# Head 1's scores ahead of the last query tile, and the sample's second value product behind the first transposition

## Chip, cores and metric

The kernel runs on one core of a Trainium2 chip. The metric is the device time of one execution in microseconds (us); the lower, the better.

## What is computed

One step of a decoder trunk of two layers, in fp32, for a prompt of 512 rows and a sample of 8 sequences of 4 new rows each; the model width is 1024, with 8 heads of 128. The second layer has the attention that the change touches. Cut to that:

```python
q = rmsnorm((xn @ att_w_q[j]).reshape(bsz, L, N_HEADS, HEAD_DIM), q_norm[j])
# prompt, per head, in blocks of 128 queries
s = einsum('bqhd,bkhd->bhqk', qb, k) * scale + cq[..., :, None] - csum[..., None, :]
p = softmax(where(causal, s, -inf));  o = einsum('bhqk,bkhd->bqhd', p, v)
# sample: 256 past keys from a paged cache and 4 new ones
p = softmax(concatenate([s_past, s_new], axis=-1))
o = einsum(p[..., :P], v_past) + einsum(p[..., P:], v_new)
mix = o.reshape(bsz, L, D_ATT) @ att_w_o[j]
```

The trunk around it (feed-forward pairs, a gated token mixer, a gated per-layer input) returns the prompt's and the sample's rows, keys, values and log forget values.

## The kernel before

All activations lie transposed on chip, 128 features by 544 columns: 512 of the prompt and 32 of the sample. A product of full precision is made of three products of split operands: each operand is cast into a high half by ScalarE (L279) and VectorE computes the rest by subtraction (L280); the same pair of lines prepares queries, turned probabilities and head outputs.

The attention is written as a list of steps, `ORDER` (L58), which a loop calls one by one. A scheduler then orders the instructions of each engine. It may move them against the list, except where an instruction is kept in program order (`keep_in_program_order`). `self.pins` says for how many of the next products the first matmul is kept so. DMA requests go out on SyncE's queue in order.

The steps that matter here, with a head, a tile or a group behind the letter:

- **q** is one query tile: 48 products of a weight block with the input (L235, L239, L241), its eviction (L949), and the square of it on ScalarE (L697).
- **s** (`s0123`, `s4567`) are the statistics of four heads: column sums of the squares on TensorE with a matrix of ones (L705), a reciprocal square root on ScalarE of each half (L334), three steps on VectorE (L337, L340, L341), and DMAs that write the rows (L716). **n** reads a head's row back, broadcast over the partitions (L721), and multiplies (L959).
- **f** requests the keys and values of a head (L992, L993); **p** splits its queries (L279, L280).
- **a** scores a head: 20 products (L1007 to L1015) into two score tiles, then for each of four query blocks of 128 the maximum on VectorE (L1025), Exp with its sum on ScalarE (L1026), the reciprocal (L1027) and the scaling on ScalarE or GpSimd (L1031, L1029). The key widths of the four blocks are 128, 256, 384 and 512. The two tiles are buffers that the next scores need, too.
- **t** turns the probabilities by ten transpositions (L1041) and splits them; **v** is the value product of 12 matmuls (L1059 to L1061), split into the head's output.
- **K**, **V**, **z**, **S**, **T** prepare the sample's keys, values, queries, scores and turned probabilities. **P** (`P0`, `P1`) is the sample's value product of a group of four sequences: 24 matmuls of 32 rows, L1124 for the past and L1129 for the new rows; eight VectorE steps (L1137, L1139) then mask the heads and sum them into one tile. **U** transposes that tile (L1143), kept in program order; **O** spreads it.
- **h** (`h00` to `h31`) is half an output projection of the first 272 columns (L1167, L1170, L1171), evicted by L1181; **o** is the projection of the other 272 columns.

There are three PSUM buffers of two banks, "ps" (query tiles, scores, turned blocks, the sample's value products, projections), and two of one bank, "pb" (square sums, the rest of a turn, value products, transpositions). The functions Exp and reciprocal square root stand in different tables of ScalarE, and an `ACT_TABLE_LOAD` changes the table.

Of the kernel before, what the change touches and what calls it, by code (L numbers as in the profile page):

```python
# [29 lines left out]
P = 128  # L30
# [10 lines left out]
NH = 8  # L41
# [16 lines left out]


ORDER = """  # L60
q0 K3 K2 K0 q1 q2 q3 K1 s0123 n2 n3 n1 q4 f1 p1 q5 q6 f0 n0 q7 p2 p0 f3 f2 a0 s4567 p3 t0 a1 v0 a2
t1 n4 a3 t2 p4 n5 n7 n6 z f4 K5 v1 v2 f5 p5 K6 t3 a4 S0 v3 f6 h00 p6 V5 f7 a5 K7 t4 K4 v4 t5 p7 V7
V3 v5 a6 x V2 h10 t6 a7 V4 S1 t7 T0 v6 V0 V1 v7 h20 V6 h30 T1 P0 h01 U0 P1 O0 h11 U1 O1 h21 h31 o0 o1 o2
o3 o4 o5 o6 o7
"""
# [18 lines left out]
def whole(p):  # L84

    return p[:].rearrange("p a b -> p (a b)")[:, 512 - CUT:512 - CUT + T]


class Builder:
# [845 lines left out]
    def queries(self, xs, acc):  # L935

        nc = self.nc
        q, sqs, bcs, box = {}, {}, {}, {}

        def tile(h):  # L940
            if h == 0:
                p, box["rstd"] = self.tile_rstd(xs, acc)
            else:
                p = self.tile_mm(xs)
            if h % 2 == 0:
                box["q"] = self.big()

            def take(p=p, qc=box["q"][:, h % 2, :]):
                box["last"] = nc.vector.tensor_tensor(qc, whole(p), box["rstd"], ALU.mult)  # L949
                q[h], sqs[h] = qc, self.square(qc)  # L950
            self.evac(take)

        def stat(*hs):
            bcs.update(zip(hs, self.head_rows([sqs.pop(h) for h in hs], P ** -0.5)))

        def norm(h):
            bc = bcs.pop(h)()
            with self.tc.issue_after(box["last"].ins):
                nc.vector.scalar_tensor_tensor(q[h], q[h], self.gain(G_Q), bc, ALU.mult, ALU.mult)  # L959
        return q, tile, stat, norm  # L960
# [21 lines left out]
    def attention(self, xs, acc, h_out, on_chunk):  # L982
        nc = self.nc
# [134 lines left out]
        def sample_pv(g):  # L1118
            pt = st.pop(("pt", g))
            acc = self.ps()  # L1120
            for a in range(2):
                for pg in range(NPAGE):
                    for b4 in range(4):
                        nc.tensor.matmul(acc[32 * b4:32 * b4 + 32, a, :],  # L1124
                                         pt[:, pg * P + 32 * b4:pg * P + 32 * b4 + 32],
                                         self.pages["V", 4 * g + b4, pg][:, a, :], start=pg == 0, stop=False,
                                         skip_group_check=True)
                for b4 in range(4):
                    nc.tensor.matmul(acc[32 * b4:32 * b4 + 32, a, :],  # L1129
                                     pt[:NS, 256 + 32 * b4:256 + 32 * b4 + 32],  # L1130
                                     st["vs"][:NS, a, :], start=False, stop=True, skip_group_check=True)
            st["oh", g] = oh = self.tmp()[:, :P]
            for h in range(NH):
                src = acc[:, h // 4, (h % 4) * P:(h % 4) * P + P]
                m = self.c[:, C_H + h:C_H + h + 1]
                if h == 0:
                    nc.vector.tensor_scalar(oh, src, m, None, ALU.mult)  # L1137
                else:
                    nc.vector.scalar_tensor_tensor(oh, src, m, oh, ALU.mult, ALU.add)  # L1139
# [45 lines left out]
        def project(c):  # L1185
# [7 lines left out]

        do = dict(q=tile, s=stat, n=norm, f=fetch, p=prep_q, a=qk, t=turn, v=pv, K=self.load_k, V=self.load_v,
                  z=sample_q, S=sample_qk, T=sample_turn, P=sample_pv, U=sample_back, O=sample_out, x=load_vs, h=project_half,
                  o=project)
        for step in ORDER.split():
# [214 lines left out]
```

## Time and profile before

| | us |
|---|---|
| median of 3 runs | 2075.44 |
| lowest to highest | 2074.86 to 2076.22 |
| the profiled execution, its own time | 2074.3 |
| its span in the trace | 2072.5 |
| TensorE busy in the span | 2043.4 (99%) |
| VectorE busy | 1509.7 (73%) |
| ScalarE busy | 941.7 (45%) |

The span begins with the first and ends with the last instruction; 1.8 us of the execution lie around it. Starts in the trace are counted from the span's start. PE is TensorE, DVE is VectorE, ACT is ScalarE, POOL is GpSimd, SP is SyncE. Of a matmul the start is known better than the end, so neighbours overlap on the timeline; an idle time stands in brackets in front of the instruction that ended it, with the engine that released it. The granted clock (PEclk) is a share of 2.4 GHz: 1.00 is that level and 0.50 is 1.2 GHz.

### The profile page before, as it was taken

The page shows a single profiled execution, that of the slowest core. Times are in us where ns is not written, and L with a number is a line of the kernel's source. Part 1 is how long each engine was busy: PE and PEld are TensorE (multiplying, and loading weights), DVE is VectorE, ACT ScalarE, POOL GpSimd, SP SyncE. Part 2 cuts the span into 40 slices and gives each one's busy share as a digit, 9 for nine tenths or more (in the row PEclk, how much of TensorE's full clock was granted, in tenths as well). Part 3 has the DMA queues.
Part 4 walks back from the last instruction along what each step waited for, and adds up shares of the span by engine and source line. Part 5 has one row for each costly group of instructions (what it writes and reads, how often), then busy time and mean ns, then how long its engine had stood idle before and what let it go on. Part 6 is the DMA issues. An engine that isn't in the chain of part 4 may idle for free. (4 is left out here: it accounts for less than half of the span.)

```text
span 2072.5 us, 38744 instructions
## 1 busy us (share of the span) xinstructions
PE 2043.4 (99%) x16388; PEld 2015.6 (97%) x16388; DVE 1509.7 (73%) x1874; ACT 941.7 (45%) x1389; POOL 180.9 (9%) x230
## 2 busy tenths in 40 slices
PE   8999999999999999999999999999999999999999
PEld 8999999999999999999999999999987999999999
DVE  7877777556687778776697777776476788777773
ACT  6535344423554434454355443534364654343451
POOL 0000000300100000052050000001142200000020
PEclk9999999999999999999999999999999999999999
DMA  5223224212223232422193323324668322322431
GB/s 184 91 104 111 74 102 155 82 44 86 87 83 113 72 112 92 140 91 92 50 333 129 112 85 110 110 67 130 198 206 305 102 102 74 111 101 84 130 96 44
DMA packets 93887, 237.94 MB, mean 115 GB/s; under 512 B 9602, under 2 KB 27554, under 8 KB 93714
## 3 DMA queue, kind: packets, MB, share of 16 engines
q1 hardware_dynamic: 93570, 235.42, 33.9%
q8 instruction: 129, 2.11, 0.4%
q14 instruction: 44, 0.36, 0.1%
q10 hardware_dynamic: 144, 0.04, 0.0%
HBM read 218.94 MB, written 16.49 MB: 114 GB/s over the span
## 5 line engine op out<-in xcount | busy, mean ns | idle before, releaser
L480 PE MATMUL ps<-big,big 128*128 128x272 f32 x5616 | 729.9, 289 | 8.1 <-DVE big L497 4.8
L480 PEld LDWEIGHTS ps<-big,big 128*128 128x128 f32 x5616 | 715.8, 189 | 9.5 <-issue 5.3
L193 DVE TENSOR_TENSOR big<-big,big 128x1024 fp32r<-128x1024 f32 (+2 forms) x538 | 590.4, 1099 | 113.7 <-ACT big L192 112.5
L192 ACT CAST big<-big 128x1024 fp32r<-128x1024 f32 (+2 forms) x538 | 488.1, 932 | 267.7 <-DVE big L178 260.2
L235 PE MATMUL ps<-big,big 128*128 128x256 f32 (+1 forms) x2832 | 590.0, 289 | 9.6 <-ACT big L192 7.0
L239 PE MATMUL ps<-big,big 128*128 128x256 f32 (+1 forms) x2832 | 584.8, 287 | 0.0
L241 PE MATMUL ps<-big,big 128*128 128x256 f32 (+1 forms) x2832 | 584.0, 288 | 0.0
L235 PEld LDWEIGHTS ps<-big,big 128*128 128x128 f32 x2832 | 453.8, 189 | 12.7 <-ACT big L192 7.0
L239 PEld LDWEIGHTS ps<-big,big 128*128 128x128 f32 x2832 | 457.0, 189 | 0.0
L241 PEld LDWEIGHTS ps<-big,big 128*128 128x128 f32 x2832 | 453.4, 188 | 0.7 <-issue 0.4
L320 POOL TENSOR_TENSOR st<-st,tmp 128x544 f32<-128x544 f32 (+1 forms) x63 | 87.2, 1384 | 1622.9 <-ACT tmp L318 1622.7
L519 DVE SCALAR_TENSOR_TENSOR big<-ps,big 128x544 f32<-128x544 f32 x160 | 115.6, 723 | 106.5 <-PE ps L241 106.3
L178 DVE TENSOR_TENSOR big<-big,big 128x1024 f32<-128x1024 f32 x156 | 190.2, 1219 | 0.3 <-DMA big<-in_w 0.3
L488 ACT COPY tmp<-ps 128x544 f32<-128x544 f32 x117 | 71.6, 612 | 141.1 <-PE ps L480 141.1
L443 ACT ACTIVATE big<-big 128x544 f32<-128x544 f32 x88 | 57.8, 660 | 159.2 <-DVE big L440 158.1
L480 PE MATMUL pb<-big,big 128*128 128x272 f32 x936 | 124.0, 288 | 0.0
L440 DVE TENSOR_TENSOR big<-big,st 128x1088 f32<-128x1088 f32 x88 | 113.0, 1290 | 10.5 <-ACT big L502 8.9
L480 PEld LDWEIGHTS pb<-big,big 128*128 128x128 f32 x936 | 120.2, 188 | 0.0
L291 ACT ACTIVATE big<-big,gains 128x544 fp32r<-128x544 f32 (+1 forms) x80 | 56.0, 705 | 121.9 <-DVE big L519 64.9
L280 DVE TENSOR_TENSOR big<-big,big 128x544 fp32r<-128x544 f32 (+1 forms) x104 | 74.6, 724 | 26.1 <-ACT big L279 25.9
L292 DVE SCALAR_TENSOR_TENSOR big<-big,gains,big 128x544 fp32r<-128x544 f32 (+1 forms) x80 | 65.1, 820 | 26.8 <-ACT big L291 26.7
L279 ACT CAST big<-big 128x544 fp32r<-128x544 f32 (+1 forms) x104 | 66.5, 644 | 29.1 <-DVE big L779 15.2
(187 smaller groups left out, 1242.7 us busy)
## 6 DMA issues: line engine op xcount, KB each, us to landing
big<-in_w SPq DMA_DIRECT2D x156, 512.0 KB
big<-in_w2a SPq DMA_DIRECT2D x64, 512.0 KB
big<-in_w2b SPq DMA_DIRECT2D x32, 384.0 KB
big<-in_w13p SPq DMA_DIRECT2D x16, 512.0 KB
big<-in_win SPq DMA_DIRECT2D x16, 512.0 KB
big<-in_wg SPq DMA_DIRECT2D x16, 512.0 KB
big<-in_wkv SPq DMA_DIRECT2D x16, 512.0 KB
big<-in_ck SPq DMA_DIRECT2D x16, 512.0 KB
```

What stands on the lines that cost most here:

```text
L178: self.nc.vector.tensor_tensor(t, a, b, ALU.add if op == "+" else ALU.subtract)
L192: self.nc.scalar.copy(hi, src)
L193: self.nc.vector.tensor_tensor(lo, src, hi.bitcast(F32), ALU.subtract)
L235: i = nc.tensor.matmul(out[:, a:b], wh, xh[:, a:b], start=s, stop=False)
L239: nc.tensor.matmul(out[:, a:b], wh, xl[:, a:b], start=False, stop=False)
L241: nc.tensor.matmul(out[:, a:b], wl, xh[:, a:b], start=False, stop=e)
L280: self.nc.vector.tensor_tensor(pair[:, 1, cols], src, pair[:, 0, cols].bitcast(F32), ALU.subtract)
L320: nc.gpsimd.tensor_tensor(acc[:, cols], acc[:, cols], sq, ALU.add)
L440: tt(g, g, rstd.unsqueeze(1).broadcast_to([P, 2, T]), ALU.mult)
L480: nc.tensor.matmul(dst[w], a[:, c], b, start=k in "152" and kp == 0 and n == 0, stop=kp == NKP - 1 and n == 2, skip_group_check=True)
L488: nc.scalar.copy(t["r" + k], t["C" if k == "5" else "A"])
L519: nc.vector.scalar_tensor_tensor(h[c], whole(out), 0.5, h[c], ALU.mult, ALU.add)
```

## The change

In `ORDER` the splitting of head 0's queries (`p0`) and the scores of head 1 (`a1`, whose queries were split first, by `p1`) move from behind `q7` to ahead of it. The turn and value product of head 1 are then called ahead of those of head 0, each in the other's place. In `tile`, the last query tile keeps its first matmul in program order, so that head 1's score products stand ahead of it on TensorE. In `sample_pv`, the first matmul of the second group is kept in program order, too, which places it behind the transposition `U0`, as the list has it. Line numbers behind the first insertion grow by one, those behind the second by five (L1026 becomes L1027, L1041 L1042, L1124 L1126, L1129 L1134, L1143 L1148, L1167 L1172).

```diff
--- before.py
+++ after.py
@@ -58,8 +58,8 @@
 
 
 ORDER = """
-q0 K3 K2 K0 q1 q2 q3 K1 s0123 n2 n3 n1 q4 f1 p1 q5 q6 f0 n0 q7 p2 p0 f3 f2 a0 s4567 p3 t0 a1 v0 a2
-t1 n4 a3 t2 p4 n5 n7 n6 z f4 K5 v1 v2 f5 p5 K6 t3 a4 S0 v3 f6 h00 p6 V5 f7 a5 K7 t4 K4 v4 t5 p7 V7
+q0 K3 K2 K0 q1 q2 q3 K1 s0123 n2 n3 n1 q4 f1 p1 q5 q6 f0 n0 p0 a1 q7 p2 f3 f2 a0 s4567 p3 t1 v1 a2
+t0 n4 a3 t2 p4 n5 n7 n6 z f4 K5 v0 v2 f5 p5 K6 t3 a4 S0 v3 f6 h00 p6 V5 f7 a5 K7 t4 K4 v4 t5 p7 V7
 V3 v5 a6 x V2 h10 t6 a7 V4 S1 t7 T0 v6 V0 V1 v7 h20 V6 h30 T1 P0 h01 U0 P1 O0 h11 U1 O1 h21 h31 o0 o1 o2
 o3 o4 o5 o6 o7
 """
@@ -938,6 +938,7 @@
         q, sqs, bcs, box = {}, {}, {}, {}
 
         def tile(h):
+            self.pins = h == NH - 1
             if h == 0:
                 p, box["rstd"] = self.tile_rstd(xs, acc)
             else:
@@ -1118,13 +1119,17 @@
         def sample_pv(g):
             pt = st.pop(("pt", g))
             acc = self.ps()
+            pin = g == 1
             for a in range(2):
                 for pg in range(NPAGE):
                     for b4 in range(4):
-                        nc.tensor.matmul(acc[32 * b4:32 * b4 + 32, a, :],
-                                         pt[:, pg * P + 32 * b4:pg * P + 32 * b4 + 32],
-                                         self.pages["V", 4 * g + b4, pg][:, a, :], start=pg == 0, stop=False,
-                                         skip_group_check=True)
+                        i = nc.tensor.matmul(acc[32 * b4:32 * b4 + 32, a, :],
+                                             pt[:, pg * P + 32 * b4:pg * P + 32 * b4 + 32],
+                                             self.pages["V", 4 * g + b4, pg][:, a, :], start=pg == 0, stop=False,
+                                             skip_group_check=True)
+                        if pin:
+                            self.tc.keep_in_program_order(i)
+                            pin = False
                 for b4 in range(4):
                     nc.tensor.matmul(acc[32 * b4:32 * b4 + 32, a, :],
                                      pt[:NS, 256 + 32 * b4:256 + 32 * b4 + 32],
```

The first place is ScalarE's queue at the first softmax. The names are buffers with a number; `st` takes the reciprocal square roots of heads 4 to 7, `pb` are their square sums, `sm` a column, `tmp` the probabilities of a query block, and `big` a split operand. Before, in the rows 932 to 941:

```order
L279 CAST big2043_16913<-big1982_16359 128x512
L334 ACTIVATE st2064_16985<-pb2062_16975,eps_78 128x272
L334 ACTIVATE st2064_16985<-pb2063_16976,eps_78 128x272
L279 CAST big2067_16998<-big1997_16545 128x512
L1026 ACT_TABLE_LOAD
L1026 ACTIVATE tmp2052_16949,sm2051_16948<-ps2048_16924,sm2050_16947 128x128
L1031 ACTIVATE tmp2052_16949<-tmp2052_16949,sm2051_16948 128x128
L1026 ACTIVATE tmp2055_16956,sm2054_16955<-ps2048_16924,sm2053_16954 128x256
L1026 ACTIVATE tmp2058_16963,sm2057_16962<-ps2049_16925,sm2056_16961 128x384
L1026 ACTIVATE tmp2061_16970,sm2060_16969<-ps2049_16925,sm2059_16968 128x512
```

After the change, at rows 941 to 950, where `ps2062` and `ps2063` are head 0's score tiles and `ps2082` the turned probabilities of head 1:

```order
L1027 ACTIVATE tmp2066_17000,sm2065_16999<-ps2062_16975,sm2064_16998 128x128
L1032 ACTIVATE tmp2066_17000<-tmp2066_17000,sm2065_16999 128x128
L279 CAST big2084_17064<-ps2082_17052 128x512
L334 ACT_TABLE_LOAD
L334 ACTIVATE st2078_17036<-pb2076_17026,eps_78 128x272
L334 ACTIVATE st2078_17036<-pb2077_17027,eps_78 128x272
L1027 ACT_TABLE_LOAD
L1027 ACTIVATE tmp2069_17007,sm2068_17006<-ps2062_16975,sm2067_17005 128x256
L1027 ACTIVATE tmp2072_17014,sm2071_17013<-ps2063_16976,sm2070_17012 128x384
L279 CAST big2085_17065<-ps2082_17052 128x384
```

Head 1's Exp, a few rows ahead of these, now uses the table of Exp before the reciprocal square roots are done, so that these stand between two table loads, and three of head 0's four Exp stand behind both.

The second place is TensorE's queue behind head 0's scores. Before, `ps2049` is head 0's second score tile, `ps2068` its turned probabilities, and `ps2073` head 1's first score tile:

```order
L1009 MATMUL ps2049_16925<-big2034_16845,big2043_16913 128x512
L1010 MATMUL ps2049_16925<-big2034_16845,big2043_16913 128x512
L1011 MATMUL ps2049_16925<-big2034_16845,big2043_16913 128x512
L1015 MATMUL ps2049_16925<-neg_107,identr_106 128x256
L1041 MATMUL ps2068_17001<-consts_104,tmp2052_16949 128x128
L1007 MATMUL ps2073_17025<-big1971_16282,big1973_16285 128x256
L1009 MATMUL ps2073_17025<-big2020_16721,big2022_16725 128x256
L1010 MATMUL ps2073_17025<-big2020_16721,big2022_16725 128x256
```

After the change, `ps2063` is head 0's second score tile, `ps2082` takes the turned probabilities of head 1, `pb2076` and `pb2077` the last of the square sums, and `ps2089` is head 2's first score tile:

```order
L1012 MATMUL ps2063_16976<-big2034_16845,big2037_16852 128x512
L1016 MATMUL ps2063_16976<-neg_107,identr_106 128x256
L1042 MATMUL ps2082_17052<-consts_104,tmp2042_16880 128x128
L1042 MATMUL ps2082_17052<-consts_104,tmp2045_16887 128x128 x2
L1042 MATMUL ps2082_17052<-consts_104,tmp2048_16894 128x128 x2
L1042 MATMUL ps2082_17052<-consts_104,tmp2051_16901 128x128 x2
L705 MATMUL pb2076_17026<-tmp2056_16962,ones_100 32x272
L705 MATMUL pb2077_17027<-tmp2056_16962,ones_100 32x272
L1008 MATMUL ps2089_17092<-big1971_16282,big1974_16286 128x256
```

Behind head 0's scores, seven transpositions of head 1 and the last square sums stand where head 0's turn and head 1's scores stood, and the next scores are head 2's.

The third place is TensorE's queue at the sample's value products. `ps2294` is the first group's product and `ps2306` the second's; `ps2296` and `ps2308` are output projections. Before:

```order
L1124 MATMUL ps2294_18313<-big2275_18149,tmp2272_18130 32x512
L1167 MATMUL ps2296_18347<-big2207_17728,big2282_18210 128x272
L1170 MATMUL ps2296_18347<-big2207_17728,big2282_18210 128x272
L1124 MATMUL ps2306_18395<-big2260_17999,tmp2293_18310 32x512
L1124 MATMUL ps2306_18395<-big2179_17569,tmp2293_18310 32x512
L1171 MATMUL ps2296_18347<-big2207_17728,big2283_18211 128x272
...
L1124 MATMUL ps2306_18395<-big2285_18242,tmp2293_18310 32x512
L1124 MATMUL ps2306_18395<-big2214_17758,tmp2293_18310 32x512
...
L1167 MATMUL ps2308_18445<-big2219_17815,big2288_18265 128x272
L1170 MATMUL ps2308_18445<-big2219_17815,big2288_18265 128x272
L1143 MATMUL pb2304_18391<-consts_104,tmp2295_18338 128x128
L1171 MATMUL ps2308_18445<-big2219_17815,big2289_18266 128x272
```

After the change:

```order
L1126 MATMUL ps2294_18313<-big2275_18149,tmp2272_18130 32x512
L1172 MATMUL ps2296_18347<-big2207_17728,big2282_18210 128x272
L1175 MATMUL ps2296_18347<-big2207_17728,big2282_18210 128x272
...
L1134 MATMUL ps2294_18313<-big2234_17868,tmp2272_18130 32x512 x4
L1172 MATMUL ps2296_18347<-big2207_17728,big2282_18210 128x272
...
L1175 MATMUL ps2296_18347<-big2280_18206,big2282_18210 128x272
L1176 MATMUL ps2296_18347<-big2280_18206,big2283_18211 128x272
L1148 MATMUL pb2304_18391<-consts_104,tmp2295_18338 128x128
L1126 MATMUL ps2306_18395<-big2260_17999,tmp2293_18310 32x512
L1126 MATMUL ps2306_18395<-big2179_17569,tmp2293_18310 32x512
```

The second product's rows, which stood inside the first product and ahead of the transposition into `pb2304`, now all stand behind that transposition, and the twelve projection products into `ps2296` are what is left between the first product and it.

## Rows read from the trace of the kernel before

**Rows 1.** Busy time of each engine, from the page: us, share, instructions.

```profile
PE 2043.4 (99%) x16388; PEld 2015.6 (97%) x16388; DVE 1509.7 (73%) x1874; ACT 941.7 (45%) x1389; POOL 180.9 (9%) x230
```

**Rows 2.** Windows: from:to, us, busy PE, PEld, DVE, ACT, POOL, PEclk, DMA, GB/s.

```profile
1500.00:1543.00 43.00, 39.32 (x362) 34.24 (x360) 31.74 (x77) 29.59 (x79) 16.41 (x33) 1.00 0.55 174
```

**Rows 3.** Waits of TensorE, 1440 to 1690: us, times, longest.

```profile
PE ps L1007 <- ACT tmp L1026: 2.1, 3, 1.3
PE ps L1167 <- DVE big L1181: 1.1, 2, 0.5
PE ps L1041 <- DVE big L1181: 0.2, 1, 0.2
```

**Rows 4.** Timeline of TensorE: start, us, instruction [idle before it <-releaser].

```profile
1498.96 1.11 PE L705 MATMUL pb<-tmp,ones 128*32 128x272 f32 x8
1500.00 0.52 PE L235 MATMUL ps<-big,big 128*128 128x256 f32 x2
1506.20 0.34 PE L1007 MATMUL ps<-big,big 128*128 128x384 f32 x1
1508.90 0.39 PE L1009 MATMUL ps<-big,big 128*128 128x256 f32 x1
1511.63 0.27 PE L1015 MATMUL ps<-neg,identr 128*128 128x256 f32 x1
```

**Rows 5.** Timeline of ScalarE around the first softmax, same columns.

```profile
1508.55 0.94 ACT L334 ACTIVATE st<-pb,eps 128x272 f32<-128x272 f32 x2
1509.39 0.61 ACT L279 CAST big<-big 128x512 fp32r<-128x512 f32 x1
1510.02 1.28 ACT L1026 ACT_TABLE_LOAD   x1
1511.32 0.37 ACT L1026 ACTIVATE tmp<-ps,sm 128x128 f32<-128x128 f32 x1
1512.33 0.47 ACT L1026 ACTIVATE tmp<-ps,sm 128x256 f32<-128x256 f32 x1
1515.07 0.69 ACT L1026 ACTIVATE tmp<-ps,sm 128x512 f32<-128x512 f32 x1 [0.82 <-DVE sm L1025]
```

**Rows 6.** Timeline of VectorE: an eviction and the statistics.

```profile
1501.55 0.72 DVE L949 TENSOR_TENSOR big<-ps,st 128x544 f32<-128x544 f32 x1
1514.95 0.74 DVE L337 SCALAR_TENSOR_TENSOR tmp<-st 128x544 f32<-128x544 f32 x1
1515.96 0.77 DVE L340 SCALAR_TENSOR_TENSOR tmp<-pb,tmp 128x272 f32<-128x272 f32 x2
```

**Rows 7.** Timeline of SyncE's queue: the request of head 4's keys.

```profile
1529.05 0.52 SPq L992 DMA_DIRECT2D big<-kd  x1
```

**Rows 8.** Timeline of TensorE, then VectorE, in the sample's value products.

```profile
1585.51 1.05 PE L1124 MATMUL ps<-big,tmp 128*32 128x512 f32 x4
1593.62 0.39 PE L1167 MATMUL ps<-big,big 128*128 128x272 f32 x1
1595.31 1.91 PE L1124 MATMUL ps<-big,tmp 128*32 128x512 f32 x12
1600.99 0.39 PE L1167 MATMUL ps<-big,big 128*128 128x272 f32 x1
1606.45 0.30 PE L1143 MATMUL pb<-consts,tmp 128*128 128x128 f32 x1 [1.27 <-DVE tmp L1139]
...
1593.83 0.35 DVE L1137 TENSOR_SCALAR tmp<-ps,consts 128x128 f32<-128x128 f32 x1 [2.27 <-PE ps L1129]
1596.95 0.73 DVE L1139 SCALAR_TENSOR_TENSOR tmp<-ps,consts,tmp 128x128 f32<-128x128 f32 x2
```

**Rows 9.** Two feed-forward gaps on TensorE's timeline; a window behind the first.

```profile
1127.94 13.84 PE L480 MATMUL ps<-big,big 128*128 128x272 f32 x96 [2.35 <-DVE big L497]
...
1683.22 8.99 PE L480 MATMUL ps<-big,big 128*128 128x272 f32 x70 [1.69 <-DVE big L497]
...
1128.00:1133.00 5.00, 5.00 (x28) 5.00 (x29) 5.00 (x7) 2.88 (x5) 0.00 (x0) 0.66 0.00 0
```

## The prediction

> **What bounds the kernel now.** I read the busy shares first. TensorE is at work for 99% of the span [rows 1], so a change can take nothing away but waits of TensorE, and must not add any. The view by stretches then says where waits are: in the 43 us from 1500 to 1543, in which the last query tiles, the first softmaxes and the first value products stand, TensorE is busy for 39.32 us, idle for 3.68, while VectorE is busy for 31.74 and ScalarE for 29.59 [rows 2]: here the softmax chain, not TensorE, ends last at several places. The list of waits names them: the score products wait for an Exp of the head before (2.1 us, three times), the output projection for its eviction (1.1, two times, and 0.2 of a transposition behind one of them) [rows 3]; in the sample's part the transposition of the second value product waits 1.27 for VectorE's masks [rows 8]. All that the change can win is in these waits; the rest of the question is what it puts in.
>
> **The change part by part.** Three things move; no product, transfer or element of work is added except what follows from the order.
>
> *Head 1's scores ahead of query tile 7.* They start where the square sums stood, at 1498.96 [rows 4]. Twenty products take about 3.3 us (from the third of head 0's to the last, 1508.90 to 1511.90, are eighteen in 3.0 [rows 4]); with a group of square sums (1.1 [rows 4]) and some 0.6 of changes between tile forms, an estimate, they end near 1503.9. Query tile 7 takes 1500.00 to 1506.20, 6.2 us [rows 4], so it ends near 1510.0. Head 1's softmax on ScalarE needs the table load, 1.28, and four Exp with their scales, which took 1511.32 to 1515.76 for head 0, 4.4 us [rows 5]. From 1502.3, when VectorE's eviction of query tile 6 ends and the square of it follows [rows 6], through 0.7 + 1.28 + 4.4, it is over near 1508.7, within the tile. The cover is 1.3 us; where it fails, head 1's transpositions wait, and they come only after head 0's scores, 4 us later. So this costs nothing.
>
> *What it does to ScalarE.* Before, the reciprocal square roots of the statistics ran ahead of the one load of Exp's table (1508.55, then 1510.02 [rows 5]). Now head 1's Exp comes ahead of them and the rest of head 0's softmax behind them: the order shows two more table loads around the pair. One load is 1.28 us, the pair 0.94 [rows 5]. In the row of the load nothing else is hidden: the cast ahead of it ends at 1510.00, the load runs 1510.02 to 1511.30, the Exp starts at 1511.32 [rows 5]. What TensorE does meanwhile: head 0's scores end near 1514.4 (3.3 and a group of square sums, 1.1, behind 1510.0), seven transpositions of head 1 (0.7) end near 1515.1, the last square sums (1.1, of query tile 7) near 1516.2. Then head 2's scores wait for a score buffer that head 0's Exp over 256 keys gives back. That Exp stands on ScalarE behind: a cast of head 1's turned block (0.6, by the casts of as many columns [rows 5]) that starts as the transpositions end, a load 1.28, the pair 0.94, a load 1.28, and its own 0.47: 4.6 us from 1515.1, so 1519.7. **TensorE waits 3.5 us** there (4.6 less the 1.1 of square sums). That is a difference of durations and hangs on none of the absolute times. Were the loads nothing it would be 0.9; it can't be under that, since the pair itself stands between.
>
> *What comes after.* VectorE's chain on the statistics (0.74, 0.77 and one more like them [rows 6]) and both heads' casts and differences are late by the same 3.5 us, and the buffers of the turned blocks and of the value products come free by these. Written forward instruction by instruction with the durations of rows 5 and 6, this gives waits of 0.65 (head 2's second score tile, for the difference of head 1's second block), 0.95 (head 1's value product, for the statistics' VectorE chain, which holds the buffers), 0.5 and 1.65 (the turns of heads 2 and 3) and 0.15 (head 4): 3.9 in all. Bounds: nothing, if ScalarE and VectorE make up the 3.5 us while TensorE stands; 3.9 if they don't. They are busy 69 and 74% of this stretch, so there is little to catch up with, and I take 3.9. With 3.5 that is 7.4 against the 3.68 of before: **+3.7**. A fourth group of square sums (each head's own, where one group of eight served two) is 0 to 1.1; the group lies between score products that otherwise changed form among query products, so I take 0. Behind this, two waits of the first output projection (0.5 of the 1.1, and the 0.2 [rows 3]) have the other head's transpositions in front of them now: **-0.7**. The same by another road: ScalarE's queue is longer by 2 × 1.28 + 0.94 = 3.5, and 0.7 is won, +2.8.
>
> On SyncE three broadcasts of statistics rows now stand ahead of head 4's keys and values, whose request went out at 1529.05 [rows 7]; with the statistics 3.5 to 4.4 us later it goes out near 1533.4. Its first reader, head 4's scores, stands near 1539; a landing within 5.6 us costs nothing, and each microsecond above it one. I take nothing: the reader is itself some 3 us late.
>
> *The sample's second value product.* Before, four of its records stood inside the first product and the rest ahead of the first one's transposition; now all of it stands behind that. Taking the four out of the middle of the first product saves what they held, 1.0 us (1.05 with what overlaps [rows 8]), and 0.2 of changes of form, an estimate. But the first transposition waits for eight VectorE masks, which take from 1593.83 to 1597.68, 3.85 us from the end of the product [rows 8], and what is left in front of it is twelve projection products, 1593.62 to 1595.31 [rows 8]: a **new wait of 2.4 us**, where 5.68 us of value product stood. The other half of the account: the second product now ends only 1.5 us later than at 1600.99 (2.4 + 0.3 of transposition less 1.2), and 24 projection products follow (3.1), to 1605.6; the second transposition waits for its own eight masks (3.85 from 1602.5), and so it runs near 1606.4, where it ran at 1606.45 with 1.27 us of waiting [rows 8]. The old wait of 1.27 and the other 0.5 of the projection [rows 3] pay the new one: **0**. Bounds: -0.9, if the second set of masks runs without the evictions and splits between (eight at 0.36 are 2.9 us, not 3.85), and +1, if they move in ahead of it.
>
> Sum: 3.7 - 0.7 + 0 = +3.0. The profiled execution was 2074.3 us (span 2072.5), so 2077.3; it stands 1.1 under the median of the three runs, 2075.44, to which I add the 3.0: **2078.4**.
>
> **The rivals.**
>
> *The clock falls in the new gaps* (slower side). A gap of 2.35 us at 1125.6 to 1127.94 was followed by a mean granted clock of 0.66 in 1128 to 1133, TensorE busy throughout, so that most of these five microseconds ran at the lower level, 1.2 GHz: 1.7 us of work lost; a gap of 1.69 ahead of 1683.22 had no such drop [rows 9]. The gap ahead of the first transposition, 2.4, lies at the upper of these, and what follows it, the second value product, is on the path to the end. Then the second masks start 1.7 later, and +3.0 becomes +4.7: 2080.1. It decides from a gap of about 2 us there, between the two rows. The gap of 3.5 at head 2 will probably cost clock as well, but TensorE waits for ScalarE and VectorE again there, which covers it.
>
> *The lag is made up* (fast side). TensorE's wait of 3.5 stands, but the five later ones vanish, as the softmaxes of heads 2 to 4 run while TensorE is behind them: 3.5 - 3.7 - 0.7 = -0.9, 2074.5. For it: ScalarE is idle for 13 us of the 43 [rows 2]. Against: its idle time lies in pieces, as the 0.8 us ahead of the last Exp of rows 5, that a lag of 3.5 can take back only as far as VectorE keeps pace.
>
> *A change of table costs more than its row.* If each of the two loads held the engine for twice its 1.28 us, 2.6 more: 2081.0. No gap in front of or behind the load's row speaks for it [rows 5]. The Trainium skill (ScalarE: Activation LUTs, What ACT_TABLE_LOAD costs) puts a switch at 1283 ns of load and about 1380 ns of drain, 2.66 us in all; by it the two switches would be 5.3 us, and the row, with 1.28 and its neighbours 0.02 away, agrees with the first part only. Its advice in the section on table sets, to batch calls by set, is what this order breaks.
>
> That the change does not do what it says can be left out: the order below shows each step moved.
>
> **How the numbers follow.** Forecast 0.40; clock 0.30; lag made up 0.18; dearer tables 0.04; something I have not seen 0.08, half to each side. The likeliest gives 2078.4. A measurement of this kernel tells a change from none at about 0.2%, 4.15 us, so from 2079.6 up it is slower, from 2071.3 down faster. The forecast's own uncertainty (the 3.9 and the two bounds of the sample part) puts 0.06 of its 0.40 above 2079.6; of the clock's 0.30, at 2080.1, somewhat over half; the dear tables wholly; with some of the unseen that is slower 0.30. Faster needs all the waits of rows 3 gone, 0.03; same 0.67. The range goes from 2074.4, which leaves out half of the made-up lag, to 2081.2, which leaves out the top of the clock case and half of the dear tables: under 0.2 outside.
>
> **What would show it.** In the changed profile: three table loads of 1.28 us between the first scores and the third softmax; a wait of TensorE of 3.5 us (3 to 4) at head 2's first score product, released by an Exp; two to four smaller ones up to the sample's first scores, which start 3.7 us later against query tile 7 and head 1 than before; no wait over 0.2 in the first output projection; 2.4 us (2 to 2.7) ahead of the first transposition of the sample's values and under 1 ahead of the second; granted clock at 1.0 behind the first of them, or 0.5 if the rival is right. The prediction is wrong if the wait at head 2 is under 2 us (the loads hidden), if the waits after it sum to under 1, if the second masks' chain runs well under or over 3.85, or if head 4's keys land late.

## The result and the profile after

The changed kernel takes 2078.67 us in the median of 17 runs (2077.20 to 2080.82), the kernel before 2074.83 in 17 (2072.17 to 2076.22): 3.8 us more by the medians, and a ratio of 1.0022 with a 95% interval of 1.0015 to 1.0028. The profiled execution of the change has a span of 2076.7 us, 4.2 more than that of before.

The list of TensorE's waits after the change, from 1440 to 1690 us (total, times, longest), answers to [rows 3]:

```profile
PE ps L1008 <- ACT tmp L1027: 3.7, 1, 3.7
PE pb L1148 <- DVE tmp L1144: 2.4, 1, 2.4
...
PE ps L1042 <- DMA tmp<-rows: 1.5, 1, 1.5
```

The waits of score products for an Exp, 2.1 us in three pieces before, are now one of 3.7. The transposition of the sample's values waits once for VectorE's masks, as before, but 2.4 us and at the other transposition. The wait of 1.5 (`L1042`) and one of 0.5 for split weights (`L1176 <- DVE L193`, shown below) are new.

ScalarE's timeline shows where the 3.7 us come from (start, duration, instruction); it answers to [rows 5]:

```profile
1503.00 1.28 ACT L1027 ACT_TABLE_LOAD   x1
...
1515.04 0.59 ACT L279 CAST big<-ps 128x512 fp32r<-128x512 f32 x1 [0.70 <-PE ps L1042]
1515.64 1.28 ACT L334 ACT_TABLE_LOAD   x1
1516.94 0.86 ACT L334 ACTIVATE st<-pb,eps 128x272 f32<-128x272 f32 x2
1517.82 1.28 ACT L1027 ACT_TABLE_LOAD   x1
1519.12 0.47 ACT L1027 ACTIVATE tmp<-ps,sm 128x256 f32<-128x256 f32 x1
```

There are three table loads of 1.28 us where one was. The second starts as the cast of head 1's turned block ends, the third as the pair of statistics ends, and only then can head 0's second Exp run, which gives TensorE its score buffer back. On TensorE's timeline, which answers to [rows 4], head 2's first score product waits for that:

```profile
1519.73 0.39 PE L1008 MATMUL ps<-big,big 128*128 128x256 f32 x1 [3.70 <-ACT tmp L1027]
...
1532.61 0.55 PE L1042 MATMUL pb<-consts,tmp 128*128 128x128 f32 x3 [0.31 <-DVE big L280]
1534.66 0.55 PE L1042 MATMUL ps<-consts,tmp 128*128 128x128 f32 x3 [1.50 <-DMA tmp<-rows]
```

The wait of 1.50 us is put down to a DMA, but that had little to do with it. VectorE's timeline shows that the difference which frees the turned block's buffer, the first of these two, ended at 1534.6, just ahead of 1534.66 (in the profile of the experiment cover the same 1.50 us are put down to that difference):

```profile
1534.06 1.14 DVE L280 TENSOR_TENSOR big<-ps,big 128x384 fp32r<-128x384 f32 x2
```

In the sample's part, TensorE's timeline, which answers to [rows 8]:

```profile
1589.03 0.39 PE L1176 MATMUL ps<-big,big 128*128 128x272 f32 x1 [0.51 <-DVE big L193]
...
1600.39 0.30 PE L1148 MATMUL pb<-consts,tmp 128*128 128x128 f32 x1 [2.45 <-DVE tmp L1144]
...
1608.60 0.39 PE L1172 MATMUL ps<-big,big 128*128 128x272 f32 x1 [0.53 <-DVE big L1186]
...
1610.50 0.30 PE L1148 MATMUL pb<-consts,tmp 128*128 128x128 f32 x1
```

and VectorE's masks there (L1142, L1144), with the split of weights ahead of them:

```profile
1587.76 2.56 DVE L193 TENSOR_TENSOR big<-big,big 128x1024 fp32r<-128x1024 f32 x2
...
1596.37 0.35 DVE L1142 TENSOR_SCALAR tmp<-ps,consts 128x128 f32<-128x128 f32 x1 [2.28 <-PE ps L1134]
...
1599.51 0.73 DVE L1144 SCALAR_TENSOR_TENSOR tmp<-ps,consts,tmp 128x128 f32<-128x128 f32 x2
...
1606.44 0.35 DVE L1142 TENSOR_SCALAR tmp<-ps,consts 128x128 f32<-128x128 f32 x1 [4.67 <-PE ps L1134]
...
1609.62 0.73 DVE L1144 SCALAR_TENSOR_TENSOR tmp<-ps,consts,tmp 128x128 f32<-128x128 f32 x2
```

Both sets of masks take 3.9 us from the end of their product, as before. The first has twelve projection products to hide behind and TensorE waits 2.45 us; the second is fully hidden, and its transposition at 1610.50 waits for nothing that counts.

The profiles differ by 1.7 us of work at a lower clock far ahead of the change, where all these kernels do the same work (last section). So the kernels are compared below by two stretches of one profiled execution each, from one fixed instruction to another: **A** from the last product of query tile 6 to the first transposition of the sample's probabilities (1498.62 to 1575.63 before, 1498.51 to 1578.54 after), and **B** from there to the first product of the feed-forward pair behind the attention (1636.59 before, 1640.77 after). Starts are subtracted; the last two columns are the timed runs.

| kernel | A, us | B, us | median, us | ratio to before (95%) |
|---|---|---|---|---|
| before | 77.01 | 60.96 | 2074.83 | |
| changed | 80.03 | 62.23 | 2078.67 | 1.0022 (1.0015 to 1.0028) |
| no_table | 77.38 | 62.23 | 2076.51 | 1.0008 (0.9999 to 1.0017) |
| order_only | 80.03 | 61.00 | 2078.42 | 1.0018 (1.0009 to 1.0027) |
| pin_only | 77.45 | 62.23 | 2077.01 | 1.0011 (1.0002 to 1.0020) |
| loads_in_before | 82.56 | 60.90 | 2078.21 | 1.0014 (1.0005 to 1.0023) |
| cover | 81.04 | 61.46 | 2077.65 | 1.0016 (1.0007 to 1.0025) |
| before_cover | 77.07 | 61.42 | 2074.74 | 0.9999 (0.9990 to 1.0008) |
| swap_one_load | 79.22 | 60.97 | 2076.36 | 1.0008 (0.9999 to 1.0017) |
| head1_cover | 78.79 | 61.46 | 2076.10 | 1.0003 (0.9994 to 1.0012) |
| no_pin_early_back | 76.92 | 60.71 | 2074.54 | 0.9998 (0.9989 to 1.0007) |
| filler | 79.67 | 62.22 | one run | |

The change costs 3.02 us in A and 1.27 in B, 4.29 together, which is the whole of the span's 4.2. Among kernels that share the rows of B, B repeats to 0.1 us; in A the four with the attention order of before (before, pin_only, before_cover, no_pin_early_back) lie between 76.92 and 77.45, so a difference of some 0.5 in A says nothing.

What the 3.02 us of A are made of, the windows show (window, us, busy PE, PEld, DVE, ACT, POOL, PEclk, DMA, GB/s), in two parts that meet at the sample's first scores; before, then changed:

```profile
1498.62:1538.66 40.04, 36.87 (x244) 31.38 (x242) 28.52 (x66) 28.02 (x70) 13.44 (x27) 1.00 0.50 163
1538.66:1575.63 36.97, 35.77 (x459) 33.47 (x459) 26.36 (x70) 24.75 (x66) 13.79 (x30) 1.00 1.05 342
...
1498.51:1543.41 44.90, 39.12 (x244) 32.87 (x242) 30.74 (x71) 32.12 (x75) 15.56 (x32) 0.96 0.51 165
1543.41:1578.54 35.13, 35.13 (x458) 33.39 (x458) 24.06 (x65) 23.70 (x64) 11.65 (x24) 1.00 1.07 348
```

Up to the sample's first scores the change loses 4.86 us, and behind them it wins 1.84. Over both parts TensorE is idle for 1.4 us more than before (5.78 against 4.37) and busy for 1.6 more; in the first part the granted clock was 0.96.

### The profile page after: what moved, and what is told of

Read it like the earlier page. It is cut to its first block, busy times and chain, and to the rows that moved or that the text cites. A ratio compares the mean times of both kernels' runs of the same rounds, so it can differ in the third digit from the quotient of the medians.

```text
span 2076.7 us, 38737 instructions
## 1 busy us (share of the span) xinstructions
PE 2044.3 (98%) x16388; PEld 2016.7 (97%) x16388; DVE 1509.9 (73%) x1874; ACT 944.5 (45%) x1391; POOL 180.0 (9%) x230
## 5 line engine op out<-in xcount | busy, mean ns | idle before, releaser
L193 DVE TENSOR_TENSOR big<-big,big 128x1024 fp32r<-128x1024 f32 (+2 forms) x538 | 590.5, 1099 | 113.2 <-ACT big L192 112.1
```

What stands on the lines that cost most here:

```text
L193: self.nc.vector.tensor_tensor(lo, src, hi.bitcast(F32), ALU.subtract)
```

## The experiments

The theory after the result: A is lost to the two table loads, with some of it to a lower clock behind the wait they cause, and B to the new wait of the first transposition. The rival: the order of the heads itself makes A's waits, and the prediction's account of B (the later wait pays) is right, so that all 4.2 us lie in A.

**No table loads.** The statistics of heads 4 to 7 use a function that every table has; nothing else moves.

```diff
-            nc.scalar.activation(r[:, a * w:(a + 1) * w], part, AF.Abs_reciprocal_sqrt, scale=1.0 / n, bias=eps)
+            nc.scalar.activation(r[:, a * w:(a + 1) * w], part, fn, scale=1.0 / n, bias=eps)
...
-            bcs.update(zip(hs, self.head_rows([sqs.pop(h) for h in hs], P ** -0.5)))
+            bcs.update(zip(hs, self.head_rows([sqs.pop(h) for h in hs], P ** -0.5, AF.Identity if 4 in hs else AF.Abs_reciprocal_sqrt)))
```

> The changed kernel in which the statistics of heads 4 to 7 use the function Identity, which every table has, in place of the reciprocal square root (their values, and so these heads' queries, are other ones); the queues are the same row for row but for two table loads less. Theory, the loads make the loss of the attention part: the wait at head 2's first score product falls from 3.7 us to about 1.4 (the pair of statistics still waits for the last square sums and takes 0.86, then Exp 0.47), no lower clock behind it, and the time is 3 to 4.5 us under the changed kernel, 0 to +1 against before. Rival, the order of the heads makes it, by the turns that stand behind each other: the wait falls, the later waits grow, and the time is at most 1.5 us under the changed kernel.

A falls from 80.03 to 77.38: 2.65 us, which is the two loads' 2.56 and hardly more (2.2 by the medians of the timed runs, whose intervals would not decide it alone). ScalarE's timeline without the loads, and TensorE's:

```profile
1516.02 0.94 ACT L334 ACTIVATE st<-pb,eps 128x272 f32<-128x272 f32 x2
1516.86 0.47 ACT L1027 ACTIVATE tmp<-ps,sm 128x256 f32<-128x256 f32 x1
```

```profile
1517.47 0.39 PE L1008 MATMUL ps<-big,big 128*128 128x256 f32 x1 [1.03 <-ACT tmp L1027]
...
1519.37 0.41 PE L1008 MATMUL ps<-big,big 128*128 128x384 f32 x1 [0.45 <-DVE big L280]
...
1525.91 0.38 PE L1061 MATMUL pb<-big,big 128*128 128x256 f32 x1 [0.47 <-DVE big L280]
```

The wait at head 2 is 1.03 (1.4 expected), but two later ones, 0.45 and 0.47, appear that the changed kernel didn't show. The windows say why. First the changed kernel (window, us, busy PE, PEld, DVE, ACT, POOL, PEclk, DMA, GB/s):

```profile
1519.70:1531.00 11.30, 11.17 (x62) 10.12 (x63) 7.88 (x24) 7.50 (x23) 4.57 (x5) 0.85 0.11 34
1521.00:1523.00 2.00, 1.94 (x7) 1.67 (x7) 1.96 (x6) 1.50 (x3) 1.12 (x1) 0.50 0.00 0
1600.00:1606.00 6.00, 5.61 (x49) 1.27 (x49) 1.67 (x3) 0.31 (x1) 2.79 (x17) 1.00 0.11 14
```

and the stretch of the first of these windows without the loads, from head 2's first score product to the same later instruction:

```profile
1517.50:1528.80 11.30, 10.26 (x63) 8.95 (x64) 7.89 (x24) 7.50 (x23) 4.57 (x5) 1.00 0.11 35
```

In the changed kernel the granted clock falls behind the wait of 3.70 us (0.50 in 1521 to 1523, the level of 1.2 GHz; 0.85 over the stretch). Without loads it stays at 1.00. Yet both stretches are 11.3 us long: TensorE is busy 11.17 us at the lower clock or 10.26 at the full one and waits for the rest. VectorE and ScalarE do the same work in both (7.88 and 7.89, 7.50 and 7.50 us): the softmax chain sets this stretch, and **the clock's fall cost nothing here**. So the theory's cause holds; its size, 3 to 4.5 us, did not, since it had counted the clock; the rival, which allowed 1.5 us at most, falls. What is left of A against before, 0.37 us, is no more than profiles of one order differ by, so in A the order of the heads costs little or nothing by itself.

**Only the order, and only the pin.** The change taken apart into the order of the attention steps and the pin, which is the first matmul of the sample's second value product kept in program order:

```diff
-            pin = g == 1
+            pin = False
```

and the kernel before with the changed `sample_pv`.

> The changed kernel without the pin in the sample's value product, so only the order of the attention steps. Theory, by the difference of the two traces: the attention part is worth +2.9 us and the pin +1.1, so this is +2.9 against before and 1.1 under the changed kernel. Rival, the prediction's account (the pin is paid by the later wait): the same time as the changed kernel, +4.

> The kernel before with the pin in the sample's value product and nothing else. Theory: +1.1 us against before, with a wait of 2.4 us ahead of the first transposition, none ahead of the second, and a new wait of 0.5 us of the projection inside the first product. Rival, the prediction's account: 0, the wait of the second transposition is under 1 and pays it.

The order alone has the change's A (80.03) and before's B (61.00); the pin alone has before's A to 0.4 and the change's B (62.23). The two parts add, and the pin costs 1.27 us. TensorE's waits in B of the order alone are those of before:

```profile
1604.92 0.39 PE L1172 MATMUL ps<-big,big 128*128 128x272 f32 x1 [0.54 <-DVE big L1186]
...
1607.97 0.30 PE L1148 MATMUL pb<-consts,tmp 128*128 128x128 f32 x1 [1.27 <-DVE tmp L1144]
```

and with the pin alone those of the change:

```profile
1586.67 0.39 PE L1175 MATMUL ps<-big,big 128*128 128x272 f32 x1 [0.51 <-DVE big L193]
...
1598.01 0.30 PE L1147 MATMUL pb<-consts,tmp 128*128 128x128 f32 x1 [2.45 <-DVE tmp L1143]
...
1606.24 0.39 PE L1171 MATMUL ps<-big,big 128*128 128x272 f32 x1 [0.53 <-DVE big L1185]
```

The third line is the eviction that the projection waited for before, too; the prediction had let it go. The first is a wait that the two early rows of the second product used to cover: the split of the next weights ends 2.4 us after the transposition of the probabilities, and products that don't need them stood just there. So the rival falls: the interval of the pin alone, 1.0002 to 1.0020, lies above 1. By the timed runs the sum is 1.8 + 1.1 thousandths against 2.2 of the change, with intervals that hold this; the medians of the change and of the order alone, only 0.25 us apart, would not have shown the pin.

**The loads in the order of before.** One activation of a single column between head 0's first and second Exp brings the table of the square root in and out again.

```diff
+                if h == 0 and i == 0:
+                    other = nc.scalar.activation(self.sm(1), self.eps, AF.Abs_reciprocal_sqrt)
+                    self.tc.keep_in_program_order(other)
```

> The kernel before with one more activation of a single column, by the reciprocal square root, between head 0's first and second Exp: it adds two table loads, 2.56 us, and about 0.2 of its own to head 0's softmax, and no other work. Theory, loads in the softmax chain are paid by TensorE: the wait of 1.3 us at head 1's second score tile becomes 4 us, a lower clock follows as behind the wait of 3.7, and the time is +2.8 to +4.6 against before. Rival, the chain has slack behind it and gives the lag back: under +1.5.

The median is 3.3 us above before (2074.92 in that comparison). In the profile, whose execution took 1.2 us more than the median, A is 5.55 longer, more than expected. ScalarE, TensorE, and a window of both behind it:

```profile
1511.97 1.28 ACT L1032 ACT_TABLE_LOAD   x1
...
1513.78 1.28 ACT L1028 ACT_TABLE_LOAD   x1
```

```profile
1513.82 0.33 PE L1048 MATMUL ps<-consts,tmp 128*128 128x128 f32 x1 [1.73 <-ACT tmp L1038]
1515.74 0.36 PE L1007 MATMUL ps<-big,big 128*128 128x256 f32 x1 [1.59 <-issue]
...
1518.64 0.69 PE L1007 MATMUL ps<-big,big 128*128 128x384 f32 x1 [1.12 <-ACT tmp L1030]
```

```profile
1515.00:1525.00 10.00, 8.14 (x40) 7.41 (x41) 5.56 (x17) 5.37 (x18) 3.09 (x3) 0.66 0.04 8
```

The loads are paid, in three waits where before had 0.55, 0.20 and 1.26: 2.4 us more. The rest is mostly the clock: 0.66 over ten microseconds, 3.4 us of work, of which little was covered here, since A's 5.55 less the waits' 2.4 leave 3.1. The rival's 1.5 is passed. By the profiles the same two loads cost more ahead of head 1's scores than ahead of head 2's; the timed runs show no such difference (3.3 us by the medians here, 3.5 for order_only).

**Fill the wait.** Eighteen transpositions of a constant in the wait at head 2 (the changed kernel otherwise; a few rows behind them move, the cast of head 1's block among them).

```diff
+            if h == 1:
+                with self.tc.issue_after(self.last_sum.ins):
+                    for _ in range(18):
+                        self.fill = nc.tensor.transpose(t[:, 1, 384:512], self.ident, self.ident)
```

> The changed kernel with 18 transpositions of a constant into an unused part of a buffer between the last square sums and head 2's scores, 2.2 us of the wait of 3.7 (the order of a few rows behind them shifts with it). Theory, the clock's fall behind that wait is covered by the softmax chain: the wait is 1.5 us and the granted clock stays 1.00, but the stretch from head 2's first score product to the sample's first scores (23.7 us in the changed kernel) is as long as before within 0.4, with more waits in it. Rival, the fall costs what it takes: 1.5 us or more less.

TensorE's timeline at the wait, and a later window:

```profile
1515.12 2.18 PE L1050 MATMUL ps<-consts 128*128 128x128 f32 x18
1517.65 0.39 PE L1008 MATMUL ps<-big,big 128*128 128x256 f32 x1 [0.34 <-ACT tmp L1030]
...
1519.80 0.44 PE L1008 MATMUL ps<-big,big 128*128 128x384 f32 x1 [0.71 <-ACT tmp L1030]
```

```profile
1533.00:1535.00 2.00, 2.00 (x7) 1.59 (x6) 2.00 (x7) 1.29 (x3) 2.00 (x5) 0.53 0.87 141
```

The fill takes 2.18 us, the wait is 0.34 and the clock stays at 1.00 behind it, but another wait comes (0.71), and further on, behind one of 1.5, the clock falls instead (0.53 in 1533 to 1535). Head 2 starts 1.24 us earlier against query tile 6 than in the changed kernel, as the cast no longer stands ahead of the loads, and A is only 0.36 shorter. From head 2's first score product to the sample's first scores it takes 24.5 us, 0.8 more than the changed kernel, so neither the 0.4 of the theory nor the gain of the rival came. That the time was not won agrees with a covered clock, but since the order moved and the clock fell elsewhere, it is weak evidence beside the run without loads.

**More cover for the first transposition.** The projection step `h11` goes ahead of it, in the changed kernel and in that of before with the pin.

```diff
-T1 P0 h01 U0 P1 O0 h11 U1 O1 h21 h31
+T1 P0 h01 h11 U0 P1 O0 h21 U1 O1 h31
```

> The changed kernel with the projection step h11 moved from behind the second value product to ahead of the first transposition, so that 34 projection products (4.3 us) stand between the first product and that transposition, where 12 did. Theory: the 2.4 us of waiting there go, the second transposition keeps 24 products in front of it (3.1 us and 0.5 of eviction) against 3.9 us of masks and waits under 0.7; the stretch from the sample's turn to the next feed-forward's products, 62.2 us in the changed kernel, is 60.0 to 61.0. Rival, the masks are shared work of VectorE and the wait only moves to the second transposition: 62 or more.

> The attention order of before, with the pin and with h11 ahead of the first transposition. Theory: the same stretch, 61.0 us before and 62.2 with the pin alone, is 60.0 to 61.0, so the time is 0 to 1 us under before. Rival: the pin's cost of 1.1 is the first product's own (the wait for split weights that the second product's rows used to cover), and cover elsewhere does not help: 61.5 or more, slower than before by 0.5.

B is 61.46 and 61.42: the wait of 2.45 is gone, and 0.8 of the pin's 1.27 us come back. TensorE's waits in the first:

```profile
1588.18 0.39 PE L1176 MATMUL ps<-big,big 128*128 128x272 f32 x1 [0.51 <-DVE big L193]
...
1599.73 0.40 PE L1172 MATMUL ps<-big,big 128*128 128x272 f32 x1 [0.81 <-DVE big L1186]
...
1609.55 0.39 PE L1172 MATMUL ps<-big,big 128*128 128x272 f32 x1 [0.54 <-DVE big L1186]
...
1613.65 0.39 PE L1172 MATMUL ps<-big,big 128*128 128x272 f32 x1 [0.53 <-DVE big L1186]
```

In place of 2.45 and 0.53 there are 0.81, 0.54 and 0.53 for evictions of the projection, which stand close behind each other now, and the 0.51 for weights stays. B lies between what the theories and the rivals expected, and neither account was right alone: cover helps, and the loss of cover inside the first product remains. A of the first is 1.0 longer than the change's, whose attention order it has; its clock fell a second time, behind the wait of 1.50, which is the likely cause. That fall, then, was not free.

**Head 1 first with one table load.** Behind query tile 7, the statistics called ahead of head 1's scores and its first Exp kept behind their square roots; then the same with the pin and the cover.

```diff
-... n0 q7 p2 p0 f3 f2 a0 s4567 p3 t0 a1 v0 a2
-t1 n4 a3 t2 p4 n5 n7 n6 z f4 K5 v1 v2 ...
+... n0 q7 p2 p0 f3 f2 s4567 a1 p3 a0 t1 v1 a2
+t0 n4 a3 t2 p4 n5 n7 n6 z f4 K5 v0 v2 ...
```

> The kernel before with head 1 scored first, but behind query tile 7, with the statistics of heads 4 to 7 called ahead of it and its first Exp kept behind their square roots, so there is one load of Exp's table as before. Theory, the change lost by the two loads and a head whose queries are split early is a gain by itself: from the last product of query tile 6 to the sample's first scores 39.0 to 40.0 us where before has 40.0 and the changed kernel 44.9. Rival, the order of the heads costs as well (without the loads the changed kernel still took 42.3): 41 to 42.5.

> Both of these in one kernel: head 1 first behind query tile 7 with one table load, the pin, and h11 ahead of the first transposition. Theory: the gains of the two add, -1 to -2 us against before. Rival: what one gives, the other part's waits take back; the same as before or slower.

TensorE's timeline of the first of the two, at head 0's second score tile:

```profile
1515.54 0.44 PE L1007 MATMUL ps<-big,big 128*128 128x384 f32 x1 [2.45 <-ACT tmp L1026]
```

The rival is right: with all statistics ahead of the first Exp, head 0's second score tile waits 2.45 us for an Exp of head 1, and the sample's first scores come after 42.1 us where before has 40.0. Together with the cover the time is that of before within its interval, A and B are each longer, and the gain of 1 to 2 us that was expected did not come. The two share the attention's order and that wait, and the clock fell behind it in the first only; its A is 0.43 longer, so there, too, most of the slower work was covered.

**No pin, the transpositions later.** Before, with the last steps called in another order.

```diff
-P0 h01 U0 P1 O0 h11 U1 O1 h21 h31
+P0 h01 P1 U0 h11 O0 h21 U1 O1 h31
```

> The attention order of before and no pin in the value product; only the last steps are called in another order: both value products, then the first transposition, then h11 and h21 (48 projection products, 6 us), and then the second transposition, with h31 behind it. The two early rows of the second product stay inside the first, where the wait for split weights is. Theory, the pin's cost is that it took away this cover and 12 products of cover were too few for 3.9 us of masks: here no transposition waits, and the stretch from the sample's turn to the next feed-forward, 61.0 us before, is 59.0 to 60.0, if the spreading of the second output (4.9 us on GpSimd) does not hold the other half of the projection, 24 products behind. Rival, it does: 60.5 to 61.5.

TensorE's waits in the last projections:

```profile
1609.68 0.39 PE L1167 MATMUL ps<-big,big 128*128 128x272 f32 x1 [0.92 <-DVE big L1181]
...
1612.68 0.39 PE L1170 MATMUL ps<-big,big 128*128 128x272 f32 x1 [0.74 <-POOL big L1155]
```

No transposition waits, as the theory said, but the projection does: 0.92 for an eviction and 0.74 for GpSimd's spreading of the second group, as the rival said. B is 60.71, 0.25 under before. No order tried here beats the kernel before by what its runs can tell.

## Why the prediction was right, step by step

- **Head 1's early scores cost nothing**: they ended at 1503.8 (1503.9 foreseen), the softmax with its scaling at 1509.0 (1508.7 foreseen; the 4.4 us taken from head 0 left out its last scaling), within query tile 7, which ended at 1509.8.
- **The wait at head 2**: 3.5 us foreseen, 3.70 measured, and its release at 1519.7 to the tenth. The chain of durations behind the transpositions was what counted: 0.59, 1.28, 0.86, 1.28, 0.47.
- **A table load costs its row**: two loads were 2.65 us in A against 2.56 in the rows. The rival of the dearer tables falls. The Trainium skill (ScalarE: Activation LUTs, What ACT_TABLE_LOAD costs) counts about 1380 ns of drain on top of each load, by which an estimate for two is 5.3 us; this case shows none of that drain. The Trainium skill's advice to batch calls by set (the same page, Table sets: the hidden batching unit) is what the change broke.
- **The later waits, 3.9 foreseen**: the profile shows 0.31, 1.50 and 0.17, where 0.5, 1.65 and 0.15 were foreseen. The foreseen 0.65 and 0.95 it does not show: TensorE ran at the lower clock through them (0.85 over 11.3 us, 1.7 us of work). Without the loads, at full clock, 0.45 and 0.47 stood in that stretch. The foreseen 7.4 us of waits were 5.8 of waits and 1.7 of slower work, which comes to the same because the softmax chain sets the time.
- **A's sum**, +3.7 - 0.7 = +3.0, was measured as 3.02, but that it fits so well is in part luck. By the prediction's own sign, the sample's first scores were to start 3.7 us later; counted from query tile 6 they start 4.9 later, and behind them 1.8 was won where 0.7 was foreseen. Of these two misses 0.51 is a wait for GpSimd that stood behind the sample's first scores before and was counted ahead of them. The rest is two things that happen to cancel: the square sums, taken at 0, took 0.64 more in four groups than in three (3.95 against 3.31), and behind the sample's first scores TensorE was busy for 0.64 less (35.13 against 35.77), which was not foreseen.
- **The clock**: the rival had it fall behind the first transposition's wait. That wait was 2.45 (2.4 foreseen), and the granted clock behind it was 1.00 in the change, no_table, pin_only and filler. It fell behind head 2's wait, where the prediction had said that the softmax chain covers it; the equal stretches of 11.3 us show that.
- **Head 4's keys** were requested at 1533.37 on SyncE's timeline (1533.4 foreseen), and no score product waited for them:

```profile
1533.37 0.52 SPq L993 DMA_DIRECT2D big<-kd  x1
```

- **The step that was mis-sized is the sample's second value product, 0 foreseen, +1.27 measured.** The new wait was right. The saving of "1.0 us" and "0.2 of changes of form" inside the first product was not: from the transposition of the second group's probabilities to the end of the twelve products it came to 0.3 us, because the rows taken out had covered a wait of 0.51 for split weights. And the "other 0.5 of the projection" was to pay as well, but it stayed (0.53 at 1608.60). The bound given for this term, +1, was too narrow by 0.3.

By this, the sum was 1.3 us short of the stretches' 4.29, and 0.8 short of the medians' 3.8. The forecast time, 2078.4, came nearer to 2078.67 than its steps, because the median of before was 0.6 lower over 17 runs than over the three that it was added to; that is luck. The interval of the ratio leaves out 1, so the change is slower. Its size lies on the prediction's line of 0.2%, at 0.19% by the medians and 0.22% by the ratio, and under the 2079.6 us from which the prediction would have called it slower.

## What to carry to other kernels

When a step is moved across engines' queues, look at the function tables: two kinds of activation that alternate in a chain that TensorE waits for cost their loads in full here (2.65 us for two rows of 1.28), although ScalarE is busy for under half of the span. Before rows of work are moved out of a place "to save a switch", see what becomes ready only while they run; here they were the cover of a weight split. And where a chain of VectorE and ScalarE sets a stretch, a lower TensorE clock in it can be free, as in the 11.3 us above, so a clock that fell is not by itself a cost; in loads_in_before, and likely in cover, it was one.

## What was not expected of the hardware

The same wait does not always bring the clock down. The feed-forward gap of 2.3 us at 1125 [rows 9], with the same work around it in every kernel here, was followed by a lower granted clock in nine of the twelve profiles and by the full clock in three; this is the window of order_only behind its gap of 2.35, to be read beside the 0.66 of [rows 9]:

```profile
1128.00:1133.00 5.00, 5.00 (x40) 5.00 (x41) 5.00 (x7) 3.16 (x6) 0.00 (x0) 1.00 0.20 33
```

It takes 1.7 us of work where it happens, beside a spread of 4 us between the runs of before; that it makes a part of this spread is likely, and not shown. The waits of 2.45 us did both, too: no fall at the first transposition in four profiles; at head 0's second score tile a fall to 0.50 in swap_one_load, and none in head1_cover. Behind the wait of 1.50 us it fell in cover and filler, and not in the change, order_only and no_table. So the prediction's bound of about 2 us, between a gap of 1.69 and one of 2.35, does not hold. What decides it is left open; it is not the length of the gap alone.
